# The order of two pairs of products, the merge of the branches and the sums of weights in a one-core attention and FFN block

## The chip, the core and the metric

The kernel runs on one core of a Trainium2 chip, in one launch. The metric is the device time of an execution in microseconds. Engines are named as the profile names them: PE (TensorE, matrix products), DVE (VectorE), ACT (ScalarE), POOL (GpSimd), and SP, whose queue here only issues DMA transfers. PEld is the loading of the stationary operand into PE.

## The reference

One layer of a streaming encoder: 512 tokens, 1024 channels, everything in float32. Two attention branches work on the same normalized input, are merged by sigmoid gates, and a gated feed-forward part with a short convolution follows.

```python
h = rmsnorm(x, norm_mix_g)
gq, gk, gv, gr, glr, fq, fk, fv, ff, g_gla, g_fox = jnp.split(h @ w_in, IN_OFFSETS, axis=-1)

log_a = log_sigmoid(glr @ gla_alpha_w2 + gla_alpha_b) / 16
o_gla = gla_chunked(gq * 64 ** -0.5, gk, gv, log_a)            # 4 heads, chunks of 64
o_gla = rmsnorm(o_gla, gla_out_norm_g) * silu(gr)

fqh, fkh = rmsnorm(fq, fox_q_norm_g), rmsnorm(fk, fox_k_norm_g)   # 8 heads of 64
o_fox = fox_attention(fqh, fkh, fv, log_sigmoid(ff + fox_forget_b))

y = sigmoid(g_gla + gate_b[0]) * (o_gla @ w_gla_branch) \
    + sigmoid(g_fox + gate_b[1]) * (o_fox @ w_fox_branch)
x = x + y @ w_out

a, val = jnp.split(rmsnorm(x, norm_ffn_g) @ w_up, 2, axis=-1)
x = x + (gelu(causal_dwconv(a, conv_w, conv_b)) * val) @ w_down
return rmsnorm(x, norm_final_g)
```

GLA is the gated linear attention (names with `g`), FoX the forgetting attention (names with `f`); `gr` is the output gate of GLA and is called `gz` in the kernel.

## The kernel before

**Exact products.** Every float32 product is made of three matmuls on a type of lower precision (`mm3`, lines 331 to 335): an operand is split into a rounded part and a remainder, and high by high, high by low and low by high are added in PSUM. Weights come from memory in pieces of 128x1024 float32, 512 KB each. Each piece is split when its turn is near (`split_next`): ACT makes `wh`, a cast of the loaded `raw` (line 298), and DVE makes `wl`, the difference of the two (line 299). Three pieces are held split at a time (`NW`). All pieces stand in one fixed list, `recipes`; a piece's number there is its time in the program.

**Fewer products.** Most large products are done by the 7 products of Strassen's method, numbered 1 to 7, over a 2x2 blocking. For this, some weights have to be added to one another. Such sums are not made by an engine: an accumulating DMA on POOL's queue adds a second matrix into the buffer (lines 306 and 310, through `dma_behind`). `dma_behind` first issues on POOL a tiny copy, `tick`, of one column of the split weights that have to be done before (line 314), and then the DMA (line 316).

**Loading.** SP issues the plain loads in the order of the list, each as soon as its buffer is free. `behind(n, "load" | "sum" | "add", ...)` ties transfers to the split of piece n. The weights of the down projection are also summed, in four arrays in memory, `wsum[0]` to `wsum[3]`: 24 copies on SP's queue (`COPY_AT`: at which piece each is issued) and 24 additions on POOL's (`ADD_AT`, `LATE_ADDS`).

**The work around the change.** In order of time:
1. The GLA inputs and four early tiles of the merge gates (`gate_tile(put_early(i))`), which are multiplied by `rb`, the factor of the first norm, and written to memory in `early` (line 692).
2. `pair_stage` (line 743), first for FoX keys and values (`kf`, `vf`), then for FoX queries and the output gate (`qf`, `gz`). One run of it computes a pair of products that share their input by Strassen's products in the order `PAIR`, 14 pieces of 12 matmuls (128x512) twice over. Product 5 comes first, its weights being a sum of two loads, then 1, 3, 6, 2, 7, 4. `pair_done` evicts: `left` is normalized per head (`qk_norm`, from `kssq` or `qssq`), `right` is scaled, and `final` is called for each of its four tiles; in the second run that is `silu` (line 870), a sigmoid on ACT, a product with it on POOL (line 873) and one into `ons`, the normalized GLA output, on DVE (line 874).
3. `fill()` lets the second run come to its end; then `transpose_heads` (line 876) transposes `ons` in two halves on PE.
4. FoX attention, with the remaining tiles of the gates put between its parts. `RUNS` tells for each key block how many steps of gate work go ahead of which part.
5. The merge (lines 1160 to 1193): for each of 8 tiles c, the two branch products are made, multiplied by the sigmoids of the gates `zg[c]` and `zf[c]`, added on POOL, and split into the operands of the output product (`halve`). The four early tiles come back from memory as `zd`.
6. The output product, whose product 5 reads a sum in the buffer `zr` (`OSUM` gives the tiles at which its load and its sum are issued), then the feed-forward part, and at its end a reload `xo<-x2d` of the residual on POOL's queue, tied by `dma_behind(last_lo, x2t, x2d)` to the split of the last large product.

The instructions are put on each engine in an order that a scheduler finds from the program; each engine then runs its own list in that order.

Of the kernel before, what the change touches and what calls it, by code (L numbers as in the profile page):

```python
# [86 lines left out]
def hybrid_kernel(ctx: ExitStack, tc, xT, xt, wp, wu, wd, wf, wn, pp, aw2, fing, out):  # L87
# [136 lines left out]
    for r in range(2):  # L224
        behind(KD + 1, "load", at_kv[5, r])
        behind(KD + 3 + r, "sum", at_kv[5, r], at_kv[1, r])
        behind(at_kv[7, r], "load", at_qr[5, r])
        behind(at_kv[2, 1] + r, "sum", at_qr[5, r], at_qr[1, r])
# [464 lines left out]
    def put_early(i):  # L693
        def put(ps):
            z = gpool.tile([P, T], F32, tag="sq", name="early", bufs=2)
            nc.vector.tensor_mul(out=z, in0=ps, in1=rb)
# [47 lines left out]
    def pair_stage(ssq, left, right, final=lambda tt: None):  # L744
        banks = {}
        for p, r in PAIR:
# [3 lines left out]
            for t2 in range(2):  # L750
                if r == 0 and new:
# [11 lines left out]
                if r == 1:  # L763
                    pair_done(p, t2, ps, ssq, left, right, final)
# [1069 lines left out]
```

## Time and profile before

| | |
|---|---|
| time, median of 3 runs | 721.43 us (719.76 to 723.34) |
| profiled execution: time / span | 720.45 / 718.7 us |
| mean granted clock of TensorE | 0.991 |
| busy: PE, DVE, ACT, POOL | 686.5, 553.7, 442.2, 153.5 us |
| idle of PE | 718.7 - 686.5 = 32.2 us |
| moved by DMA | 149.05 MB, 207 GB/s on average |

The span is the time from the first to the last instruction of the profiled execution. PE is busy nearly throughout, so the places of interest are the gaps in its work. In the timeline a row has start and duration, engine, line, operation, output and inputs with their shapes, and in brackets the idle time of the engine just before it and who ended it. The line of a weight split is always 298 or 299, so what it belongs to follows from the time and the buffer.

### The profile page before, as it was taken

How to read it: one execution, taken by the hardware profiler on the slowest of the kernel's cores; microseconds unless marked ns; L12 is line 12 of the kernel's file. 1: busy time of each engine (PE TensorE's matmuls, PEld its weight loads, DVE VectorE, ACT ScalarE, POOL GpSimd, SP SyncE). 2: the span in 40 equal slices, each digit the busy share in tenths (PEclk: the TensorE clock that was granted, in tenths of full speed). 3: DMA queues.
4: the chain of work that ended last, by engine and by line, in shares of the span. 5: the costliest groups of instructions: out<-in, count | busy, mean ns of one | idle time of the engine just before them, and what ended most of it. 6: DMA issues, size and time to landing. Idle time of an engine off the chain costs nothing.

```text
span 718.7 us, 10670 instructions
## 1 busy us (share of the span) xinstructions
PE 686.5 (96%) x3851; PEld 583.1 (81%) x3851; DVE 553.7 (77%) x876; ACT 442.2 (62%) x712; POOL 153.5 (21%) x206
## 2 busy tenths in 40 slices
PE   9999999897899999998899999999999999799996
PEld 6788888685678877876788999999999998588885
DVE  6776858679567776558769999888989879667884
ACT  8487374556767877624575766665665567355663
POOL 1134111104232211433100122111121204400112
PEclk9999999999999999999999999999999999899999
DMA  8789959875767767687895689999999988986543
GB/s 316 267 219 314 306 113 246 175 196 136 202 182 188 197 151 184 171 231 190 216 285 142 135 205 208 234 223 217 202 206 206 215 186 233 305 251 201 176 148 117
DMA packets 48633, 149.05 MB, mean 207 GB/s; under 512 B 5668, under 2 KB 9660, under 8 KB 48452
## 3 DMA queue, kind: packets, MB, share of 16 engines
q1 hardware_dynamic: 32452, 95.61, 38.9%
q0 software_dynamic: 12960, 47.72, 37.3%
q10 hardware_dynamic: 3168, 5.05, 2.0%
q8 instruction: 30, 0.49, 0.3%
q14 instruction: 23, 0.19, 0.1%
HBM read 143.09 MB, written 28.33 MB: 239 GB/s over the span
## 4 chain that ended last, share of the span: by engine, by line
PE 68%; DVE 10%; DMA 9%; ACT 8%; issue 3%; POOL 2%; DVEq 0%; ACTq 0%; POOLq 0%
PE ps_mm L334 12%; PE ps_mm L333 12%; PE ps_mm L335 12%; PE ps_wide L1476 8%; PE ps_wide L1478 4%; PE ps_wide L333 4%; PE ps_wide L335 4%; PE ps_wide L334 4%; DMA zr<-in_wp_dram 4%; DVE wl L299 4%; ACT wh L298 2%; DMA early<-early 2%; DMA rawp<-in_wp_dram 1%; ACT pr L1016 1%; DMA xo<-x2d 1%
## 5 line engine op out<-in xcount | busy, mean ns | idle before, releaser
L298 ACT CAST wh<-rawx 128x1024 fp32r<-128x1024 f32 x75 | 76.0, 1013 | 60.9 <-PE ps_mm L334 32.3
L333 PE MATMUL ps_mm<-xw,wh 128*128 128x256 f32 (+1 forms) x296 | 101.0, 341 | 0.1
L334 PE MATMUL ps_mm<-xw,wh 128*128 128x256 f32 (+1 forms) x296 | 99.2, 335 | 0.0
L335 PE MATMUL ps_mm<-xw,wl 128*128 128x256 f32 (+1 forms) x296 | 99.1, 335 | 0.0
L299 DVE TENSOR_TENSOR wl<-rawx,wh 128x1024 fp32r<-128x1024 f32 x75 | 88.2, 1177 | 12.9 <-ACT wh L298 12.9
L299 DVE TENSOR_TENSOR wl<-raw,wh 128x1024 fp32r<-128x1024 f32 x58 | 71.4, 1233 | 11.6 <-ACT wh L298 10.6
L298 ACT CAST wh<-raw 128x1024 fp32r<-128x1024 f32 x58 | 60.8, 1049 | 25.2 <-PE ps_mm L335 9.6
L333 PEld LDWEIGHTS ps_mm<-xw,wh 128*128 128x128 f32 x296 | 56.7, 192 | 7.4 <-issue 1.4
L335 PEld LDWEIGHTS ps_mm<-xw,wl 128*128 128x128 f32 x296 | 56.7, 191 | 5.6
L334 PEld LDWEIGHTS ps_mm<-xw,wh 128*128 128x128 f32 x296 | 56.7, 192 | 5.1 <-DVE xw L1265 0.2
L299 DVE TENSOR_TENSOR wl<-rawz,wh 128x1024 fp32r<-128x1024 f32 x31 | 38.1, 1233 | 16.1 <-ACT wh L298 16.0
L306 POOL DMA_DIRECT2D rawx<-in_wu_dram x30 | 26.0, 867 | 111.6 <-DVE wl L299 76.8
L1476 PE MATMUL ps_wide<-xo,wh 128*128 128x512 f32 x192 | 48.1, 392 | 0.0
L334 PE MATMUL ps_mm<-wl,xw 128*128 128x512 f32 x88 | 35.8, 407 | 6.8 <-DVE wl L299 6.8
L333 PE MATMUL ps_mm<-xc,wh 128*128 128x256 f32 (+1 forms) x128 | 42.0, 328 | 0.0
L334 PE MATMUL ps_mm<-xc,wh 128*128 128x256 f32 (+1 forms) x128 | 41.5, 324 | 0.0
L335 PE MATMUL ps_mm<-xc,wl 128*128 128x256 f32 (+1 forms) x128 | 41.4, 324 | 0.0
L314 POOL COPY tick<-wl 128x1 f32<-128x1 f32 x38 | 19.8, 520 | 100.4 <-DVE wl L299 98.0
L298 ACT CAST wh<-rawz 128x1024 fp32r<-128x1024 f32 x31 | 32.3, 1046 | 12.6 <-PE ps_mm L335 6.5
L1476 PEld LDWEIGHTS ps_wide<-xo,wh 128*128 128x128 f32 x192 | 34.5, 189 | 6.2
L335 PE MATMUL ps_mm<-wh,xw 128*128 128x512 f32 x88 | 35.3, 401 | 0.0
L333 PE MATMUL ps_mm<-wh,xw 128*128 128x512 f32 x88 | 35.1, 400 | 0.0
(500 smaller groups left out, 1871.2 us busy)
## 6 DMA issues: line engine op xcount, KB each, us to landing
rawx<-in_wu_dram POOLq DMA_DIRECT2D x40, 512.0 KB, 7.2
rawz<-in_wp_dram SPq DMA_DIRECT2D x30, 512.0 KB, 6.3
raw<-in_wp_dram SPq DMA_DIRECT2D x20, 512.0 KB, 4.7
wsum<-in_wd_dram SPq DMA_DIRECT2D x20, 512.0 KB, 9.2
rawx<-in_wu_dram SPq DMA_DIRECT2D x20, 512.0 KB, 4.7
raw<-in_wu_dram SPq DMA_DIRECT2D x20, 512.0 KB, 5.0
rawx<-wsum SPq DMA_DIRECT2D x12, 512.0 KB, 4.5
wsum<-in_wd_dram POOLq DMA_DIRECT2D x10, 512.0 KB, 8.7
```

The costliest lines, as they stand in the source:

```text
L298: nc.scalar.copy(out=hi[:, :m], in_=raw[:, :m])
L299: last_split[:] = [nc.vector.tensor_sub(out=lo[:, :m], in0=raw[:, :m], in1=hi[:, :m].bitcast(F32))]
L306: nc.gpsimd.dma_start(raw, recipes[i][0], accum_op=ALU.add)
L314: now = nc.gpsimd.tensor_copy(out=tick, in_=lo[:, 0:1].bitcast(F32))
L333: mm(ps, lhsT=ah, rhs=bh, start=start, stop=False, **k)
L334: mm(ps, lhsT=ah, rhs=bl, start=False, stop=False, **k)
L335: mm(ps, lhsT=al, rhs=bh, start=False, stop=stop, **k)
L1016: nc.scalar.activation(out=p, in_=p, func=AF.Exp, scale=-1.0, bias=nm, accum_out=rs)
L1476: mm(ps[:, i], lhsT=wh[:, c], rhs=both[p][:, k], start=first and k == 0, stop=False, skip_group_check=True)
L1478: mm(ps[:, i, 0], lhsT=wl[:, c], rhs=both[p][:, k, 0], start=False, stop=k == KH - 1, skip_group_check=True,)
```

## The change

The change is in which pair comes first, in when things are merged and summed, and in the engine of one eviction. No product is added or left out.

1. **Pairs.** FoX queries and output gate come first, keys and values second. The second run has the order `PAIR2`: product 1 ahead of product 5. The PSUM banks of the first two sets are taken at the start of a run.
2. **Heads.** `silu` runs in the first of the two runs. The transposes of `ons` are put into the second run, the first half after 2 of its steps and the other after 6 more (`HEADS_AT`).
3. **Early gates.** `put_early` copies with ACT; the product with `rb` is made on DVE when a tile comes back, at the start of the merge.
4. **RUNS.** In two entries one step of gate work moves from ahead of a part to behind it.
5. **Sums of the down weights.** The last 6 copies are issued at pieces 20 to 22 (before: 44 to 54). The last 6 additions, which were issued at the last pieces of the program, go to pieces 56 to 63; the 18 others are spread over 44 to 55.
6. **Merge.** The sum and the splits of tile c-1 are issued behind the products of tile c. The loads and sums of `zr` move from tiles 4, 5, 6, 7 to 5, 6, 6, 7.

```diff
-    (7, "t2", 3, "v0", 3, "t3"),
+    (6, "t2", 4, "v0", 3, "t3"),
...
-    (7, "t8", 3, "v2", 3, "t9"),
+    (6, "t8", 4, "v2", 3, "t9"),
...
+HEADS_AT = (2, 6)
...
-COPY_AT = [8 + i * 2 // 3 for i in range(18)] + [44 + 2 * i for i in range(6)]
-ADD_AT = [44 + i for i in range(12)] + [56 + i * 3 // 2 for i in range(6)]
-LATE_ADDS = 6
+COPY_AT = [8 + i * 2 // 3 for i in range(18)] + [20 + i // 2 for i in range(6)]
+ADD_AT = [44 + i * 2 // 3 for i in range(18)] + [56 + i * 3 // 2 for i in range(6)]
...
-OSUM = (4, 5)
+OSUM = (5, 6)
 PAIR = ((5, 0), (5, 1), (1, 0), (1, 1), (3, 0), (3, 1), (6, 0), (6, 1), (2, 0), (7, 0), (7, 1), (2, 1), (4, 0), (4, 1))
+PAIR2 = PAIR[2:4] + PAIR[:2] + PAIR[4:]
...
-    at_kv = pair_recipes(16, 12, ("rawz", "rawp", "raw"))
-    at_qr = pair_recipes(20, 8, ("rawz", "raw", "rawp"))
+    at_qr = pair_recipes(20, 8, ("rawz", "rawp", "raw"), PAIR)
+    at_kv = pair_recipes(16, 12, ("rawz", "raw", "rawp"), PAIR2)
...
-        behind(at_branch[OSUM[0] + 2 * r], "load", at_out[5, r])
-        behind(at_branch[OSUM[1] + 2 * r], "sum", at_out[5, r], at_out[1, r])
+        behind(at_branch[OSUM[0] + r], "load", at_out[5, r])
+        behind(at_branch[OSUM[1] + r], "sum", at_out[5, r], at_out[1, r])
...
-    parts_at([at_last[1 + i] for i in range(LATE_ADDS)], adds_at, ((3, wsum[1]),))
...
-            nc.vector.tensor_mul(out=z, in0=ps, in1=rb)
+            nc.scalar.copy(out=z, in_=ps)
...
-        banks = {}
-        for p, r in PAIR:
+        banks = {name: [pmm() for _ in range(2)] for name in "zx"}
+        for p, r in pair:
...
-    work += [gate_tile(put_early(i)) for i in range(NEARLY)] + [pair_stage(kssq, kf, vf)]
+    work += [gate_tile(put_early(i)) for i in range(NEARLY)] + [
+        pair_stage(PAIR, qssq, qf, lambda: late["gz"], silu)
+    ]
...
-    work += [pair_stage(qssq, qf, gz, silu)]
+    fill(18)
+    work += [pair_stage(PAIR2, kssq, kf, lambda: vf)]
+    for u in range(2):
+        fill(HEADS_AT[u])
+        transpose_heads(u)
     fill()
-    for u in range(2):
-        transpose_heads(u)
...
         nc.sync.dma_start(zg[i], early[:, i])
+        nc.vector.tensor_mul(out=zg[i], in0=zg[i], in1=rb)
...
+        if c > 0:
+            merge(c - 1)
         if c in HELD:
             held.append(piece())
+    merge(KD - 1)
```

Three places show what the scheduler made of it. The first is PE around the end of the second run of `pair_stage`. Of the kernel before, the rows show the last gate matmuls ahead of the attention, with the second half of the transposes of `ons` (the first half stands 17 matmuls ahead, right behind the run's last matmul):

```order
L334 MATMUL ps_mm<-xw,wh 128x512
L882 MATMUL ps_ax<-ident,ons 128x128 x8
L335 MATMUL ps_mm<-xw,wl 128x512
L333 MATMUL ps_mm<-xc_110,wh 128x512
L334 MATMUL ps_mm<-xc_110,wh 128x512
L335 MATMUL ps_mm<-xc_110,wl 128x512
L333 MATMUL ps_mm<-xc_111,wh 128x512
L334 MATMUL ps_mm<-xc_111,wh 128x512
L335 MATMUL ps_mm<-xc_111,wl 128x512
L967 MATMUL ps_lg<-ident,kf 128x128 x4
L977 MATMUL ps_lg<-ident,qf 128x128 x4
L1004 MATMUL ps_lg<-kh,qh 128x128 x2
```

Of the change, the same place (the transposes of `kf` and `qf` now have 12 gate matmuls on either side):

```order
L333 MATMUL ps_mm<-xw,wh 128x512
L334 MATMUL ps_mm<-xw,wl 128x512
L972 MATMUL ps_lg<-ident,kf 128x128 x4
L982 MATMUL ps_lg<-ident,qf 128x128 x4
L332 MATMUL ps_mm<-xw,wh 128x512
L333 MATMUL ps_mm<-xw,wh 128x512
```

And of the change, the second half of the transposes of `ons` inside the second run (the matmuls around it are those of `pair_stage`):

```order
L332 MATMUL ps_mm<-wh,htz 128x512
L333 MATMUL ps_mm<-wl,htz 128x512
L334 MATMUL ps_mm<-wh,lmz 128x512
L885 MATMUL ps_ax<-ident,ons 128x128 x8
L332 MATMUL ps_mm<-wh,hqg 128x512
L333 MATMUL ps_mm<-wl,hqg 128x512
```

The transposes have left the place ahead of the attention.

The second place is DVE at the start of the merge; `ogl` are the remainders of the transposed GLA output, which PE's first products of the merge read. Before:

```order
L1159 TENSOR_TENSOR held<-ogr_115,ogh_2922 128x512
L1159 TENSOR_TENSOR ogl_2946<-ogr_116,ogh_2923 128x512
L955 TENSOR_TENSOR zg_1702<-ps_mm,rb 128x512
L1159 TENSOR_TENSOR ogl_2949<-ogr_117,ogh_2924 128x512
L299 TENSOR_TENSOR wl<-raw,wh 128x1024
L1159 TENSOR_TENSOR ogl_2952<-ogr_118,ogh_2925 128x512
```

In the change:

```order
L1165 TENSOR_TENSOR held<-ogr_115,ogh_2934 128x512
L1165 TENSOR_TENSOR ogl_2962<-ogr_116,ogh_2935 128x512
L960 TENSOR_TENSOR zg_1709<-ps_mm,rb 128x512
L1165 TENSOR_TENSOR ogl_2965<-ogr_117,ogh_2936 128x512
L1159 TENSOR_TENSOR zd<-zd,rb 128x512
L1165 TENSOR_TENSOR ogl_2968<-ogr_118,ogh_2937 128x512
L1159 TENSOR_TENSOR zd<-zd,rb 128x512 x3
L298 TENSOR_TENSOR wl<-raw,wh 128x1024
L1200 TENSOR_TENSOR zd<-ps_mm,zd 128x512
```

Four products of `zd` with `rb` have come in, the first of them ahead of the last `ogl`; the split `wl` has gone behind them.

The third place is the end of POOL's list: what follows the last accumulating DMA into the up weights (`wsum3` is the last array of sums, `wl_6004` in the list before and `wl_6020` in the changed one the split that `last_lo` names). Before:

```order
L306 DMA rawx_5546<-in_wu_dram 128x1024
L314 COPY tick_90<-wl_5984 128x1
L316 DMA wsum3_72<-wsum1_70 128x1024
L314 COPY tick_90<-wl_6044 128x1
L316 DMA wsum3_72<-wsum1_70 128x1024
L314 COPY tick_90<-wl_6064 128x1
L316 DMA wsum3_72<-wsum1_70 128x1024
L314 COPY tick_90<-wl_6004 128x1
L316 DMA xo2_6100<-x2d_2918 128x4096
L314 COPY tick_90<-wl_6004 128x1
L316 DMA xo2_6100<-in_fing_dram 128x1024
L314 COPY tick_90<-wl_6106 128x1
```

In the change:

```order
L305 DMA rawx_5564<-in_wu_dram 128x1024
L313 COPY tick_90<-wl_6020 128x1
L315 DMA xo2_6112<-x2d_2930 128x4096
L313 COPY tick_90<-wl_6020 128x1
L315 DMA xo2_6112<-in_fing_dram 128x1024
```

The additions into `wsum3` have left this place, and the reload of the residual follows the up weights directly.

More of the change, by code (lines that the diff above doesn't have):

```diff
@@ L224, in hybrid_kernel @@
     for r in range(2):
[L225 to L228, printed above, removed]
+        behind(KD + 1, "load", at_qr[5, r])
+        behind(KD + 3 + r, "sum", at_qr[5, r], at_qr[1, r])
+        behind(at_qr[7, r], "load", at_kv[5, r])
+        behind(at_qr[2, 1] + r, "sum", at_kv[5, r], at_kv[1, r])
         for at in (at_kv, at_qr):
@@ L742, in pair_operand, with pair_stage @@
         return xh[j * K2 + k][:, t], xl[j * K2 + k][:, t]
-    def pair_stage(ssq, left, right, final=lambda tt: None):
-        banks = {}
-        for p, r in PAIR:
+    def pair_stage(pair, ssq, left, right, final=lambda tt: None):
+        banks = {name: [pmm() for _ in range(2)] for name in "zx"}
+        for p, r in pair:
             name = {5: "z", 3: "z", 1: "x", 2: "x", 6: "y", 7: "y", 4: "y"}[p]
@@ L750, in pair_stage @@
             for t2 in range(2):
-                if r == 0 and new:
+                if r == 0 and p == 6:
                     banks.setdefault(name, []).append(pmm())
@@ L763, in pair_stage @@
                 if r == 1:
[L764 removed]
+                    pair_done(p, t2, ps, ssq, left, right(), final)
                 yield
@@ L795, in pair_done, with silu @@
             final(2 + t2)
+    def silu(tt):
+        gz, ons = late["gz"], late["ons"]
+        sg = gpool.tile([P, 512], F32, tag="sq", name="sg", bufs=2)
+        nc.scalar.activation(out=sg, in_=gz[:, tt], func=AF.Sigmoid)
+        nc.gpsimd.tensor_mul(out=sg, in0=gz[:, tt], in1=sg)
+        nc.vector.tensor_mul(out=ons[:, tt], in0=ons[:, tt], in1=sg)
     for qb in range(NT):
@@ L868, in hybrid_kernel @@
             pair_split((3, 6, 7)[tt], last_dve, ("qg", "kg", "fgs")[tt], ("e2", None, None)[tt])
-    def silu(tt):
-        sg = gpool.tile([P, 512], F32, tag="sq", name="sg", bufs=2)
-        nc.scalar.activation(out=sg, in_=gz[:, tt], func=AF.Sigmoid)
-        nc.gpsimd.tensor_mul(out=sg, in0=gz[:, tt], in1=sg)
-        nc.vector.tensor_mul(out=ons[:, tt], in0=ons[:, tt], in1=sg)
     def transpose_heads(u):
@@ L904, in hybrid_kernel @@
                 )
+    late["gz"] = gpool.tile([P, NT, 512], F32, tag="vg", name="gz")
     for u in range(2):
@@ L924, in hybrid_kernel @@
     rsqrt_mean(rg, gssq.rearrange("p u a b c -> p (u a b c)"), 16, 1.0 / GDV, gpool, "rg")
-    ons = gpool.tile([P, NT, 512], F32, tag="prev", name="ons")
+    ons = late["ons"] = gpool.tile([P, NT, 512], F32, tag="prev", name="ons")
     for u in range(2):
@@ L1160, in hybrid_kernel, with merge @@
     held = []
-    for c in range(KD):
-        w = piece()
-        pg = pmm()
-        feature_tile(pg, w, ogh, ogl, nk=GH)
-        pf = pmm()
-        feature_tile(pf, w, oth, otl, w0=GH, nk=GH)
+    def merge(c):
         z = zf[c]
-        sigmoid(zg[c], zg[c], bias=col(C_GB + c))
-        last_sigmoid = sigmoid(z, z, bias=col(C_GB + KD + c))
-        nc.vector.tensor_mul(out=zg[c], in0=pg, in1=zg[c])
-        nc.vector.tensor_mul(out=z, in0=pf, in1=z)
         if c < KD // 2:
@@ L1191, in hybrid_kernel @@
             halve(o24, k, z)
+    for c in range(KD):
+        w = piece()
+        pg = pmm()
+        feature_tile(pg, w, ogh, ogl, nk=GH)
+        pf = pmm()
+        feature_tile(pf, w, oth, otl, w0=GH, nk=GH)
+        z = zf[c]
+        sigmoid(zg[c], zg[c], bias=col(C_GB + c))
+        last_sigmoid = sigmoid(z, z, bias=col(C_GB + KD + c))
+        nc.vector.tensor_mul(out=zg[c], in0=pg, in1=zg[c])
+        nc.vector.tensor_mul(out=z, in0=pf, in1=z)
+        if c > 0:
+            merge(c - 1)
         if c in HELD:
             held.append(piece())
+    merge(KD - 1)
     x2 = [[opool.tile([P, T], F32, tag="ot", name="x2t", bufs=2 * GH) for _ in range(2)] for _ in range(NT)]
```

6 lines of the change are left out of this document (3 added, 3 removed).

## The prediction

> **What bounds the kernel now.** I read the first part of the page, then the list of who waited for whom on TensorE, then the timelines of the engines around each wait.
>
> ```profile
> PE 686.5 (96%) x3851; PEld 583.1 (81%) x3851; DVE 553.7 (77%) x876; ACT 442.2 (62%) x712; POOL 153.5 (21%) x206
> PE ps_mm L334 <- DVE wl L299: 8.4, 5, 3.7
> PE ps_ax L882 <- DVE ons L874: 5.3, 2, 3.3
> PE ps_mm L333 <- DVE zg L1170: 2.1, 2, 1.3
> PE ps_lg L1063 <- DVE pl L1045: 1.8, 2, 0.9
> ```
>
> TensorE is busy 686.5 of 718.7 us, so everything that can be won without taking matmuls away lies in 718.7 - 686.5 = 32.2 us of idle time, and in the stretches where its clock is low. The change keeps the number of large matmuls. The question is therefore which of the waits above it ends, and which new ones it makes. The four rows (us in total, times, longest) hold 17.6 of the 32.2 us. They belong to five places, taken in order of time below, with rows of the timeline: start and duration in us, the instruction, and in brackets the idle time before it and what ended it. All sums are made against the profiled execution, 720.45 us with a span of 718.7; that execution is 1 us below the median of the runs shown (721.43), inside their spread.
>
> **1. The early gates, 60 to 90 us.** Four evictions of early gate tiles move from VectorE, as products with `rb`, to ScalarE, as copies.
>
> ```profile
> 84.66 0.69 DVE L696 TENSOR_TENSOR early<-ps_mm,rb 128x512 f32<-128x512 f32 x1 [0.71 <-DMA early<-early]
> 87.15 0.68 PE L900 MATMUL ps_ax<-vg,sc 128*128 128x128 f32 x4 [0.95 <-DVE prev L863]
> ```
>
> The last of them holds VectorE for 0.71 + 0.69 us, ahead of the chain of `prev`, for which TensorE waits 0.95 us. Taken off that queue, 1.4 us are freed and the 0.95 us should go: **-0.9** (0 to -0.95). ScalarE pays four copies of 0.67 us (the 2.67 for four of that size in section 4); it is busy 62% of the span and nothing of TensorE waits for it here.
>
> **2. From the first half of the pair work to the second.** Before, the second stage starts with product 5, whose weights are the sum of two loads.
>
> ```profile
> 126.96 0.50 PE L334 MATMUL ps_mm<-wl,htz 128*128 128x512 f32 x1 [0.81 <-DVE wl L299]
> 130.78 0.50 PE L334 MATMUL ps_mm<-wl,htz 128*128 128x512 f32 x1 [0.80 <-DVE wl L299]
> 135.43 0.50 PE L334 MATMUL ps_mm<-wl,xw 128*128 128x512 f32 x1 [1.63 <-DVE wl L299]
> 128.36 1.06 ACT L298 CAST wh<-rawp 128x1024 fp32r<-128x1024 f32 x1 [2.77 <-DMA rawp<-in_wp_dram]
> ```
>
> Three waits, 3.24 us, and the ScalarE row shows why: the cast waited 2.77 us for the accumulating DMA into `rawp`. With `PAIR2` the stage starts with product 1, a plain load, and the two sums are wanted two pieces later. That is 24 matmuls, 5.0 us by the window of 605 to 610 below, against 2.77 of lateness, so the DMA is covered. But the split of the first piece now stands on VectorE behind the first product of `silu`, which waits for POOL. The nearest row is the 1.63 above, a split held up in VectorE's queue. I take one such wait a little shorter, 1.4, and one of 0.5 us in place of the three: **-1.3** (from -3.2 to +1.5, three waits of 1.6 each).
>
> **3. From the second half to the logits, 168 to 190 us.**
>
> ```profile
> 170.43 0.88 PE L882 MATMUL ps_ax<-ident,ons 128*128 128x128 f32 x6 [2.03 <-DVE ons L874]
> 178.48 1.17 PE L882 MATMUL ps_ax<-ident,ons 128*128 128x128 f32 x8 [3.27 <-DVE ons L874]
> 183.71 0.33 PE L1004 MATMUL ps_lg<-kh,qh 64*128 64x128 f32 x2 [1.56 <-ACT qh L979]
> 172.71 2.81 POOL L873 TENSOR_TENSOR sg<-gz,sg 128x512 f32<-128x512 f32 x2
> 172.33 3.23 DVE L376 TENSOR_TENSOR rq16w<-rq16w,rq16v 128x16 f32<-128x16 f32 x1
> 171.70 0.17 DVE L376 TENSOR_TENSOR rq16w<-rq16w,rq16v 128x16 f32<-128x16 f32 x1
> 166.12 0.67 DVE L670 TENSOR_REDUCE qssq<-fsq 128x8 f32<-128x512 f32 x1
> 163.80 2.40 DVE L680 TENSOR_TENSOR qf<-qf,rq 128x512 f32<-128x512 f32 x2
> 168.02 0.38 PE L882 MATMUL ps_ax<-ident,ons 128*128 128x128 f32 x2
> 176.44 1.29 DVE L680 TENSOR_TENSOR qf<-qf,rq 128x512 f32<-128x512 f32 x2
> 185.00:190.00 5.00, 4.85 (x24) 3.91 (x25) 2.74 (x16) 3.58 (x10) 0.20 (x1) 0.69 1.03 248
> ```
>
> At the end of stage 2 TensorE waits 2.03 + 3.27 us for `ons`, that is for sigmoid, POOL's product and VectorE's product of the last tiles, and then 1.56 us for `qh`, whose norm ran late in the same queues. VectorE's tiny step of 0.17 us took 3.23 at 172.33, beside POOL's two products (2.81). In the change these products belong to stage 1, and the transposes are taken in the middle of stage 2, after 2 and then 6 more steps, with 12 or more matmuls ahead of each, so `ons` is no longer waited for (some 2.5 us of cover per 12 matmuls). What stays is the norm of the keys. VectorE has two splits left ahead of it, ten steps of about 0.2 us and the products (1.29 for two). From the last sum of squares (done at 166.79, and 1.1 us sooner without POOL beside it, since the product at 163.80 took 2.40 where 1.29 is its time) that is 2.4 + 2.1 + 1.3 = 5.8 us: the norm is done at 171.5. Stage 2 ends at 168.02 and 12 gate matmuls cover 2.5, to 170.5. I take 1.0 us in place of 2.03 + 3.27 + 1.56 and the 0.7 of two short waits behind: **-6.5** (-4.5 to -7.5). The last row is of the view by windows (busy us of the five engines, then granted clock, DMA share, GB/s) and shows a granted 0.69 for the 5 us after these waits; (1 - 0.69) x 5 = 1.6 us. With nothing longer than 1 us ahead, that goes: **-1.6** (0 to -1.6).
>
> **4. The merge, 280 to 346 us.** Here the change adds a wait.
>
> ```profile
> 280.20 2.92 SPq L1153 DMA_DIRECT2D zd<-early  x4
> 287.66 2.67 ACT L1149 ACTIVATE zd<-zd,ppt 128x512 f32<-128x512 f32 x4 [3.15 <-DMA zd<-early]
> 285.26 0.68 DVE L1159 TENSOR_TENSOR ogl<-ogr,ogh 128x512 fp32r<-128x512 f32 x1
> 286.00 0.51 PE L334 MATMUL ps_mm<-ogl,wh 128*128 128x512 f32 x1 [0.52 <-DVE ogl L1159]
> 312.55 0.90 POOL L316 DMA_DIRECT2D zr<-in_wp_dram  x1 [6.76 <-DMA zr<-in_wp_dram]
> 317.73 0.47 PE L333 MATMUL ps_mm<-ogh,wh 128*128 128x512 f32 x1 [1.27 <-DVE zg L1170]
> ```
>
> The product with `rb` is now made when the early tiles come back, and the first of the four stands on VectorE ahead of the last `ogl`. The tiles land at about 287.6 (ScalarE's first row that was released by them). The product takes 0.69, `ogl` 0.68: TensorE, which needs `ogl` and stood from 285.48 (286.00 - 0.52), goes on at about 289.0. That is 3.5 us of idle in place of 0.52: **+3.0**. Would the clock fall too? After 3.27 and then 1.56 us of idle it fell to 0.69 (section 3), after 3.71 to 0.50 (section 5); after 2.03 alone no window fell. 3.5 lies between, so I count 2 us: **+2.0** (0 to 2.5). In the Trainium skill, "TensorE: Matmul & The Clock Gate", section "HAM oscillation — how this bites in real kernels", the rule is no idle gap of TensorE over some 3.4 us; by it this wait, worked out at 3.5, would cost the low clock, and by the page the sum keeps the 2 us. It speaks against this part of the change; the trace agrees as far as 3.71 did and 2.03 did not.
>
> In exchange, POOL stood 6.76 us behind the load of `zr`, with the sum of the fourth tile queued behind it; that made the 1.27, and 0.85, 0.22, 0.61 and 0.28 after it, 3.2 us in the same chain. The sums of the tiles now come ahead of that queue entry, and each merge has one more tile (5.4 us) to finish. I count **-4.5**: these 3.2 and some of the 1.7 us at the first product of the output weights. Bounds -1 and -5; the net of the merge is +0.5 (-2 to +4.5).
>
> **5. The tail, 594 to 635 us.** Six additions into the down weights leave POOL's queue here.
>
> ```profile
> 605.10 0.51 POOL L314 COPY tick<-wl 128x1 f32<-128x1 f32 x1 [2.47 <-DVE wl L299]
> 606.08 7.54 POOL L314 COPY tick<-wl 128x1 f32<-128x1 f32 x1
> 613.57 0.58 POOL L316 DMA_DIRECT2D xo<-x2d  x1
> 614.37 1.23 DVE L299 TENSOR_TENSOR wl<-raw,wh 128x1024 fp32r<-128x1024 f32 x1 [0.79 <-POOL tick L314]
> 615.67 1.23 DVE L299 TENSOR_TENSOR wl<-rawx,wh 128x1024 fp32r<-128x1024 f32 x1
> 622.39 1.29 DVE L1674 TENSOR_TENSOR xo<-xo,ps_wide 128x512 f32<-128x512 f32 x2 [5.49 <-DMA xo<-x2d]
> 615.65 0.50 PE L334 MATMUL ps_mm<-wl,xw 128*128 128x512 f32 x1 [1.49 <-DVE wl L299]
> 624.87 0.80 PE L334 MATMUL ps_mm<-wl,xw 128*128 128x512 f32 x1 [3.71 <-DVE wl L299]
> 605.00:610.00 5.00, 5.00 (x24) 4.14 (x23) 5.00 (x8) 2.67 (x6) 4.90 (x3) 1.00 1.02 243
> 625.00:630.00 5.00, 5.00 (x12) 3.95 (x13) 3.62 (x5) 0.46 (x1) 0.00 (x0) 0.50 1.06 246
> ```
>
> The reload `xo<-x2d` stands on POOL behind three of the additions. Its tick copy then took 7.54 us beside a VectorE that was busy for all of 605 to 610, the load went out at 613.57 and VectorE stood 5.49 us for it, with the next split behind: 3.71 us of TensorE, and 12 matmuls in the next 5 us where there are 24 at full clock, 2.5 us. Without the additions the same tick is due as soon as its split is done, some 7 us sooner. If it takes the 0.5 of the tick at 605.10, the load is issued by 602 and lands by 611 (8.7 us to landing, 622.39 - 613.57), ahead of 616.90, where VectorE wants it. The 0.79 at 614.37, a split behind that tick, goes as well. **-3.7 - 2.5 - 0.8 = -7.0** (0 to -7.0). The additions themselves run earlier, on other pieces of POOL's queue, at 0.5 us a tick.
>
> **6. What I count at nothing.** Two entries of `RUNS` move one step of filling from ahead of one run to behind the next: the same work stands ahead of what follows, and the 1.8 us of waits for `pl` hang on a chain of VectorE: 0 (-1.8, both gone, to +0.9, one more). Six copies into the down weights, 0.5 MB each, move to pieces 20 to 22.
>
> ```profile
> 95.00:100.00 5.00, 5.00 (x23) 4.13 (x22) 4.73 (x12) 3.69 (x5) 0.86 (x1) 1.00 0.17 16
> 105.00:110.00 5.00, 5.00 (x24) 4.14 (x23) 3.35 (x4) 2.24 (x3) 0.00 (x0) 1.00 1.06 198
> ```
>
> The DMA engines are 0.17 busy at 95 to 100 us, which is cover for half of the 3 MB (15 us at the 198 GB/s of the second row); from 105 on they are full. TensorE waits for no load there now. I take 0 (to +10).
>
> **Sum.** -0.9 - 1.3 - 6.5 - 1.6 + 0.5 - 7.0 = -16.8, so 720.45 - 16.8 = 703.7 us; I say 704.
>
> **The rivals.**
> - *The tick is starved all the same.* VectorE is as busy at 598 to 613 as before, and a tick took 7.54 us there; against it, the one at 605.10 took 0.51 in the same stretch. Then the load goes out near 613 again, the 7.0 us are lost, and the time is 711. The Trainium skill, "SBUF — State Buffer", section "SBUF: two separate sides", has VectorE and GpSimd share one pair of ports under an exclusive lock; by it a copy on POOL may wait for a run of VectorE's two-input operations, and the 7.54 us agree, while the 0.51 does not.
> - *The merge gives more back.* The wait for the early tiles falls on a later landing, TensorE's clock falls, and the loads of `zr`, of which there are now two in a chain, hold SP and the output pieces: the net is +4.5 in place of +0.5, so 708.
> - *The heads do not leave the path.* The transposes in stage 2 wait for `ons` as they did, with the same POOL products: half of the 8.1 us of section 3 stays, 708.
> - *Slower.* The six copies stand on SP ahead of the loads of the pair pieces. If these 3 MB, 15 us of full DMA, fall behind 105 us instead of the gap, the pieces' loads come late by up to 15 us, less the 3 to 5 us that they are ahead now: 10 us in stage 1, and again in stage 2, whose sums are accumulated on top of those buffers. Each such wait also costs the low clock, 2.5 us. 2 x 12.5 = 25 against 16.8: 728. It decides once pieces land over 9 us late; the 0.17 speaks against it.
>
> **How the numbers follow.** My case 0.68, at 704 with its bounds 697 to 708; starved tick 0.13, at 711; merge 0.07 and heads 0.05, at 708; slower 0.07, at 728 if it is full, near no change if half. The range of 697 to 714 takes in all but the last, with 3 us over the starved tick for copies that come a little late. A measurement of this kernel can tell about 0.5%, 3.6 us: faster by more than that 0.89, within it 0.05, slower 0.06.
>
> **What would show it.** Right: no wait for `ons` and clock 1.00 through the start of the logits; the `xo` load issued before 605 or so and no TensorE wait over 1 us after 610; one wait of 3 to 4 us for `ogl` at the merge's start, and no 6.76 on POOL ahead of the fourth tile. Wrong: a tick of several us on POOL near 600; splits in stages 1 and 2 that wait for DMA; a second wait in the merge as long as the first.

## The result, and the profile after

The changed kernel takes 711.3 us (median; 708.3 to 712.5) against 720.6 us before: a ratio of 0.9864, interval 0.9816 to 0.9912. That is 9.3 us faster, inside the range given, but little over half of the 16.8 us that were worked out. The profiled execution, at 712.52 us with a span of 710.8, is the slowest of the four; sums over stages and waits are made in its time below, and for every other run in that of its own profiled execution.

The first part of the page and the list of who waited for whom on TensorE (us in total, times, longest) now read:

```profile
PE 686.8 (97%) x3851; PEld 585.7 (82%) x3851; DVE 553.3 (78%) x876; ACT 444.6 (63%) x716; POOL 147.8 (21%) x206
PE ps_mm L333 <- DVE ogl L1165: 3.8, 2, 3.5
PE ps_mm L332 <- DVE zg L1200: 3.4, 1, 3.4
PE ps_lg L1068 <- DVE pl L1050: 2.5, 2, 1.6
PE ps_lg L1068 <- ACT ph L1049: 2.0, 1, 2.0
PE ps_mm L333 <- DVE wl L298: 2.0, 2, 1.3
```

The 5.3 us for `ons` and most of the 8.4 us for `wl` are gone. At the head of the list stand waits that the kernel before did not have or had at 0.5 to 1.3 us. TensorE's busy time is the same, but busy time counts matmuls at the low clock as well: three stretches now run at it (195 to 210, 280 to 290 and 325 to 340 us), where the kernel before has two (185 to 195 and 620 to 635). The rows of the timeline of TensorE that cut the run into four, for the kernel before:

```profile
281.42 0.51 PE L333 MATMUL ps_mm<-ogh,wh 128*128 128x512 f32 x1
345.92 0.51 PE L334 MATMUL ps_ax<-wl,oh 128*128 128x512 f32 x1 [0.76 <-DVE wl L299]
```

and for the changed one:

```profile
174.23 0.33 PE L1009 MATMUL ps_lg<-kh,qh 64*128 64x128 f32 x2
274.40 0.51 PE L332 MATMUL ps_mm<-ogh,wh 128*128 128x512 f32 x1
346.30 0.50 PE L333 MATMUL ps_ax<-wl,oh 128*128 128x512 f32 x1 [0.76 <-DVE wl L298]
```

The first logits stood at 183.71 before. So the spans of the four stages, and what the prediction had for each, are:

| stage | before | after | measured | predicted |
|---|---|---|---|---|
| to the first logits | 183.71 | 174.23 | -9.5 | -0.9 - 1.3 - 6.5 = -8.7 |
| attention, to the first product of the merge | 97.71 | 100.17 | +2.5 | -1.6 |
| merge, to the output product's second piece of a split | 64.50 | 71.90 | +7.4 | +0.5 |
| from there to the end | 372.78 | 364.50 | -8.3 | -7.0 |
| sum | 718.7 | 710.8 | -7.9 | -16.8 |

Two stages did what was expected, and 2.1 us more in all; the two others missed it by 11 us. The experiments below look for the cause of each.

### The profile page after: what moved, and what is told of

Same layout as the page of the kernel before. It is cut to its first block, busy times and chain, and to the rows that moved or that the text cites. A ratio compares the mean times of both kernels' runs of the same rounds, so it can differ in the third digit from the quotient of the medians.

```text
span 710.8 us, 10664 instructions
## 1 busy us (share of the span) xinstructions
PE 686.8 (97%) x3851; PEld 585.7 (82%) x3851; DVE 553.3 (78%) x876; ACT 444.6 (63%) x716; POOL 147.8 (21%) x206
## 4 chain that ended last, share of the span: by engine, by line
PE 74%; DMA 9%; DVE 8%; ACT 4%; issue 3%; POOL 2%; SPq 0%; ACTq 0%; POOLq 0%; DVEq 0%
PE ps_mm L332 14%; PE ps_mm L333 14%; PE ps_mm L334 13%; PE ps_wide L1489 8%; PE ps_wide L332 4%; PE ps_wide L333 4%; PE ps_wide L334 4%; PE ps_wide L1491 4%; DMA zr<-in_wp_dram 4%; DMA cb<-nct 4%; DVE wl L298 3%; PE ps_lg L1068 1%; ACT pr L1021 1%; ACT wh L297 1%; DMA zd<-early 1%
## 5 line engine op out<-in xcount | busy, mean ns | idle before, releaser
L313 POOL COPY tick<-wl 128x1 f32<-128x1 f32 x38 | 13.8, 362 | 114.7 <-DVE wl L298 113.5
L332 PE MATMUL ps_mm<-wh,xw 128*128 128x512 f32 x88 | 34.3, 390 | 0.0
L334 PE MATMUL ps_mm<-wh,xw 128*128 128x512 f32 x88 | 34.3, 389 | 0.0
```

The costliest lines, as they stand in the source:

```text
L313: now = nc.gpsimd.tensor_copy(out=tick, in_=lo[:, 0:1].bitcast(F32))
L332: mm(ps, lhsT=ah, rhs=bh, start=start, stop=False, **k)
L334: mm(ps, lhsT=al, rhs=bh, start=False, stop=stop, **k)
```

## The experiments

Each of the first four takes the changed kernel and edits one part of it.

**The product with `rb` behind the last `ogl`.**

```diff
     for i in range(NEARLY):
         zg[i] = bpool.tile([P, T], F32, tag="zd", name="zd", bufs=NEARLY)
         nc.sync.dma_start(zg[i], early[:, i])
-        nc.vector.tensor_mul(out=zg[i], in0=zg[i], in1=rb)
...
-        nc.vector.tensor_sub(out=ogl[h], in0=ogr[h], in1=ogh[h].bitcast(F32))
+        last_ogl = nc.vector.tensor_sub(out=ogl[h], in0=ogr[h], in1=ogh[h].bitcast(F32))
+    for i in range(NEARLY):
+        with tc.issue_after(last_ogl.ins):
+            nc.vector.tensor_mul(out=zg[i], in0=zg[i], in1=rb)
```

> The changed kernel (711.3 us) with one edit: the four products of the early tiles with rb are made behind the last ogl on VectorE, no longer ahead of it. Theory: the 3.47 us wait for ogl at the merge's start and the low clock behind it (0.58 and 0.73 in the two windows of 5 us) are the price of that one product's place; the wait falls to 0.5 us or so, the clock stays at 1.00, and the time falls by 3.0 + 2 to 3 = 5 to 6 us, to 705.5. Rival: the first sigmoid needs the same early tile, so the wait only moves to the first merge products; TensorE stands as long at the second or third tile and the time stays within 2 us of 711.3.

Measured: 703.7 us (ratio to before 0.9728, 0.9695 to 0.976), 7.6 us below the changed kernel. In the changed kernel the timelines of VectorE and TensorE and the view by windows (busy us of five engines, granted clock, DMA share, GB/s) show what the place costs:

```profile
280.33 0.69 DVE L1159 TENSOR_TENSOR zd<-zd,rb 128x512 f32<-128x512 f32 x1 [3.14 <-DMA zd<-early]
280.94 0.68 DVE L1165 TENSOR_TENSOR ogl<-ogr,ogh 128x512 fp32r<-128x512 f32 x1
281.68 0.80 PE L333 MATMUL ps_mm<-ogl,wh 128*128 128x512 f32 x1 [3.47 <-DVE ogl L1165]
280.00:285.00 5.00, 3.32 (x8) 2.65 (x9) 4.67 (x7) 3.94 (x7) 0.00 (x0) 0.58 0.27 105
285.00:290.00 5.00, 5.00 (x18) 3.99 (x17) 0.86 (x2) 1.55 (x2) 1.27 (x1) 0.73 0.31 107
```

VectorE stood 3.14 us for the early tile with `ogl` behind it, TensorE 3.47. With the edit:

```profile
280.28 0.50 PE L333 MATMUL ps_mm<-ogl,wh 128*128 128x512 f32 x1 [0.54 <-DVE ogl L1164]
280.00:285.00 5.00, 4.72 (x21) 3.88 (x22) 3.89 (x7) 3.73 (x7) 0.00 (x0) 1.00 0.74 281
```

The wait and the low clock are gone, and the wait does not turn up later: the products with `rb` had time behind `ogl`. The second wait of the merge (3.43 us for `zg`) went as well, which had not been expected from this edit; 0.59 us of it is left. So the 7.6 us are the price of both waits, not of the first alone.

**One load into `zr` instead of two.** Each of the two pieces that go into `zr` is loaded once by the look-ahead and once more by its own entry. (SP issues four loads into `zr` in the changed kernel; in the kernel before it issued three, at 300.97, 315.77 and 321.30 us.)

```diff
             if what == "load":
-                load_raw(i)
+                if i not in raws:
+                    load_raw(i)
```

> The changed kernel with one edit: a load that has been issued already is not issued again (two of the four loads into zr are left out; they bring in the same weights twice). Theory: POOL stands 6.30 and 8.57 us for the second load of each pair, and the sums of tiles 4 and 5 behind it; without them the sums are made in time, the 3.43 us wait for zg at 329.5 and the half clock behind it (0.50 in one window) go, and the time falls by 3.4 + 2.5 = 6 us, to 705.5. Rival: POOL stands for the first load as well, because SP issues it late; then one wait of 6 us stays on POOL and TensorE's wait falls by less than half, to 709 or so.

Measured: 705.5 us (0.9755, 0.9714 to 0.9797). SP's, POOL's and TensorE's timelines of the changed kernel:

```profile
297.87 12.97 SPq L268 DMA_DIRECT2D zr<-in_wp_dram  x2
314.35 0.90 POOL L315 DMA_DIRECT2D zr<-in_wp_dram  x1 [6.30 <-DMA zr<-in_wp_dram]
318.80 0.33 SPq L268 DMA_DIRECT2D zr<-in_wp_dram  x1
325.27 0.88 POOL L315 DMA_DIRECT2D zr<-in_wp_dram  x1 [8.57 <-DMA zr<-in_wp_dram]
325.88 1.56 POOL L1179 TENSOR_TENSOR zg<-zg,zg 128x512 f32<-128x512 f32 x1
329.47 0.80 PE L332 MATMUL ps_mm<-held,oh 128*128 128x512 f32 x1 [3.43 <-DVE zg L1200]
330.00:335.00 5.00, 5.00 (x13) 3.63 (x12) 3.39 (x6) 2.27 (x4) 2.85 (x2) 0.50 0.50 98
```

The last load into `zr` is issued at 318.80, and POOL stands for its landing until 325.27. The sum of tile 5 (the sixth; tiles count from 0) runs behind that, and VectorE and TensorE behind the sum. With the second loads left out, POOL's two entries read:

```profile
311.17 0.90 POOL L316 DMA_DIRECT2D zr<-in_wp_dram  x1 [2.63 <-DMA zr<-in_wp_dram]
313.81 0.88 POOL L316 DMA_DIRECT2D zr<-in_wp_dram  x1 [0.17 <-issue]
```

and TensorE has no wait for `zg` at all, though the first wait of the merge (3.70 us) is still there. So either edit ends the second wait. In the first experiment the same four loads still hold POOL for 3.12 and 6.38 us, and are over by 315.93. But the chain of loads and the first wait together are not the whole cause: the next two experiments keep both, and the second wait is shorter in them. How the first wait makes the chain longer was not tried apart.

**The additions at their old density.**

```diff
-ADD_AT = [44 + i * 2 // 3 for i in range(18)] + [56 + i * 3 // 2 for i in range(6)]
+ADD_AT = [44 + i for i in range(12)] + [56 + i * 3 // 2 for i in range(6)]
...
-    parts_at(ADD_AT, adds_at, ((0, b11), (2, b12), (1, wsum[0]), (3, wsum[1])))
+    parts_at(ADD_AT, adds_at, ((0, b11), (2, b12), (1, wsum[0])))
...
+    parts_at([at_step[4 + i, 1] for i in range(6)], adds_at, ((3, wsum[1]),))
```

> The changed kernel with the additions into the down weights at the density of before: 12 at pieces 44 to 55, 6 at 56 to 63, and the last 6 in the middle of the feed-forward part instead of near the end. Theory: the waits for ph and pl at 198.6 and 200.7 us (2.04 + 1.59) come from the loads of cb, 15.3 us to landing beside five additions; with fewer additions these loads land in 9 to 11 us, the waits fall to 1 us, the clock stays at 1.00 (now 0.50 for 5 us), and the time falls by 2.6 + 2.5 = 5 us, to 706. Rival: the loads of cb are late because they are issued late and wanted sooner, whatever runs beside them; the waits stay at 3 us or more and the time within 1.5 us of 711.3.

The last six, which have no place at the old density, go into the feed-forward part. Measured: 708.6 us (0.98, 0.9755 to 0.9844); its runs (705.1 to 711.4) overlap with those of the changed kernel (708.3 to 712.5), so what the edit does is read from the profile. In the changed kernel, POOL's and TensorE's timelines and one window in the attention read:

```profile
188.10 0.42 POOL L638 TENSOR_TENSOR cb<-cb,negm 128x128 f32<-128x128 f32 x1 [10.25 <-DMA cb<-nct]
193.75 1.41 POOL L638 TENSOR_TENSOR cb<-cb,negm 128x128 f32<-128x128 f32 x3 [1.30 <-DMA cb<-nct]
198.60 0.54 PE L1068 MATMUL ps_lg<-ph,v 128*128 128x512 f32 x1 [2.04 <-ACT ph L1049]
200.73 0.80 PE L1068 MATMUL ps_lg<-pl,v 128*128 128x512 f32 x1 [1.59 <-DVE pl L1050]
200.00:205.00 5.00, 4.27 (x15) 3.99 (x16) 2.29 (x5) 0.89 (x2) 1.36 (x3) 0.50 1.04 234
```

With the additions at the old density (four of them between 166 and 178 us, where the changed kernel has six):

```profile
188.47 1.98 POOL L640 TENSOR_TENSOR cb<-cb,negm 128x128 f32<-128x128 f32 x5 [0.41 <-DMA cb<-nct]
198.09 0.50 PE L1070 MATMUL ps_lg<-pl,v 128*128 128x512 f32 x1 [0.87 <-DVE pl L1052]
200.00:205.00 5.00, 5.00 (x34) 3.99 (x33) 4.68 (x8) 3.60 (x7) 1.81 (x5) 1.00 0.51 111
```

The last of the six sums of `cb` ends at 190.45 (188.47 + 1.98) in place of 195.16, the wait for `ph` is gone and `pl` is back at the 0.87 of before. The loads of `cb` of 192 and 128 KB that are issued from 177 us on take 10.4 us to landing, where they take 15.3 in the changed kernel and in the kernel before 8.3 and 8.6. For these waits the mechanism is the one expected. The time fell by 2.7 us and not by 5, and the edit did more than was expected of it, which the profiled execution (705.1, the fastest of the four) shows: the attention is 4.8 us shorter, the part from the output product on, in which six additions now stand, 2.0 us longer, and the merge 4.7 us shorter. There the first wait is still 3.17 us and POOL waits 4.52 and 7.15 us for the loads of `zr`, but the second wait has shrunk without a low clock:

```profile
PE ps_mm L334 <- DVE zg L1203: 1.6, 2, 1.0
330.00:335.00 5.00, 4.04 (x16) 2.49 (x15) 3.66 (x8) 3.01 (x6) 0.67 (x1) 1.00 1.00 306
```

Which of these gains the slower three executions lack is open.

**The old `RUNS`.**

```diff
-    (6, "t2", 4, "v0", 3, "t3"),
+    (7, "t2", 3, "v0", 3, "t3"),
...
-    (6, "t8", 4, "v2", 3, "t9"),
+    (7, "t8", 3, "v2", 3, "t9"),
```

> The changed kernel with the old RUNS: one step of gate work (three matmuls, 0.7 us) goes back in front of t2 and of t8. Theory: the total of work ahead of v0 and v2 is the same, and the waits for ph and pl hang on the loads of cb; the time is unchanged, 711.3 within 1 us. Rival: the move of RUNS is what brings TensorE to v0 too early; then the waits at 198.6 and 200.7 shrink by at least half and the clock stays up, 707.

Measured: 709.7 us (0.9808, 0.9772 to 0.9844), 1.6 us below the changed kernel and inside the spread of its runs. The waits for `ph` (1.9 us) and `pl` (2.8 in all) stay: `RUNS` is not what makes them. The first wait of the merge stays too (3.45 us), but the second is 1.93 and 0.99 us with the clock at 1.00, though POOL still waits 6.12 and 7.15 us for the loads of `zr`; the last landing holds POOL until 322.74 in place of 325.27. So a landing 2.5 us earlier went with a shorter wait in two parts and no low clock.

**All three edits together**, with the six additions in the feed-forward part.

> The changed kernel with the edits of e1, e2 and e3 together. Theory: three separate losses (the place of one product with rb; the density of the additions beside the loads of cb; the second load into zr). e1 measured 703.7, which also ended the second merge wait (0.6 us left), so e2 adds little to e1; e3's part is the waits at v0 (2.46 + 1.79 in e1's profile, against 0.9 at old density) and 5 us at a clock of 0.56: 3.3 + 2.5 us. The time is 703.7 - 5.5 = 698, TensorE's mean clock 0.995 or more. Rival: the places share one cause (an overlap of DMA traffic, or the clock), so the gains don't add up: 702 or more.

Measured: 697.5 us (0.9673, 0.9616 to 0.973), below both kernels. The time is the 698 that was expected. The three gains taken singly are 7.6 + 5.8 + 2.7 = 16.1 us, against 13.8 together, since each of the three edits ends or shortens the same second wait. No window of 5 us ahead of the end has a clock below 0.985.

The next three take the kernel before and add one part of the change, or the changed kernel and leave all but one.

**The tail alone**, in the kernel before:

```diff
-    parts_at([at_last[1 + i] for i in range(LATE_ADDS)], adds_at, ((3, wsum[1]),))
+    parts_at([at_step[4 + i, 1] for i in range(LATE_ADDS)], adds_at, ((3, wsum[1]),))
```

> The kernel before with one edit: the last 6 additions into the down weights are issued in the middle of the feed-forward part, no longer at its end. Theory: the 7.54 us tick ahead of the reload of the residual, 3.71 + 0.79 us of TensorE and 2.5 us of low clock hang on these additions alone; the ratio to before is (720.5 - 7.0) / 720.5 = 0.990, and the reload is issued by 605 us. Rival: VectorE's run of work starves the tick as it did, the reload goes out past 612 us, and the ratio is 0.998 or more.

Measured: 717.1 us (0.9939, 0.9904 to 0.9974), half of the 7 us. The reload was issued at 605.51 and both waits of the tail are gone, but new waits stand where the additions went: 0.72 and 0.47 us for splits at 521 and 533, 1.32 for `joint` at 540, 2.5 us in all.

**The pairs and heads alone** (parts 3 to 6 of the change undone).

```diff
-            nc.scalar.copy(out=z, in_=ps)
+            nc.vector.tensor_mul(out=z, in0=ps, in1=rb)
...
-OSUM = (5, 6)
+OSUM = (4, 5)
...
-        if c > 0:
-            merge(c - 1)
...
-    merge(KD - 1)
...
+    parts_at([at_last[1 + i] for i in range(LATE_ADDS)], adds_at, ((3, wsum[1]),))
```

> The changed kernel with parts 3 to 6 of the change undone: only the order of the pairs and the place of the heads differ from before. Theory: the three waits between the pairs shrink from 3.24 to 2.0 us, the waits ahead of the logits from 7.5 to 0.3 us, and the low clock behind them goes (1.6 us): 10 us in all, less what the loads of cb cost because the attention starts sooner (0 to 3 us at the old density of the additions); a ratio of 0.986 to 0.990. Rival: the whole gain of this part is given back in the attention, which has its own pace from the loads of cb on; a ratio of 0.995 or more.

Measured: 710.1 us (0.9861, 0.9796 to 0.9926): by itself this part is worth as much as the whole change. The waits between the pairs are 1.35 and 0.63, none over 0.45 us stands between them and the logits, and the attention waits 0.91 + 0.98 us at `v0` against 2.04 + 1.59 with the denser additions. With the early products still on VectorE, its profile shows a wait of 4.24 us for `prev` at 90.55. The profiled execution, at 714.77, is the slowest of the four; the others took 709.8 to 710.4, so that wait need not be in them.

**The later merge alone**, in the kernel before.

```diff
-OSUM = (4, 5)
+OSUM = (5, 6)
...
+        if c > 0:
+            merge(c - 1)
...
+    merge(KD - 1)
```

> The kernel before with part 6 of the change alone: the merge of a tile one tile later, loads and sums of zr at tiles 5, 6, 6, 7. Theory: without the product with rb in front of ogl, this removes the 1.27 + 0.85 + 0.22 us at the merge and some of the waits at the first output products, 2 to 3 us, a ratio of 0.996 or so. Rival: the second load of zr that this part adds holds POOL for 6 to 8 us even so, a wait for zg of 2 us or more takes the place of the 1.27, and the ratio is 1.000 or above.

Measured: 720.35 us, ratio 1.0001 (0.9964 to 1.0037), the rival's figure. POOL stands 3.95 and 6.66 us for the loads of `zr`, and TensorE waits 1.06, 0.98 and 0.59 us for `zg` in place of 1.27, 0.85 and 0.22: no single wait of 2 us, as the rival had it, but no less in all.

The last four look for the best place for the additions. All have the edits of the first two experiments and the old density elsewhere.

**Beside the output product.**

```diff
-    parts_at([at_step[4 + i, 1] for i in range(6)], adds_at, ((3, wsum[1]),))
+    parts_at([66 + 2 * i for i in range(6)], adds_at, ((3, wsum[1]),))
```

> e5 (697.5 us) with the last 6 additions at pieces 66, 68 to 76, beside the output product, in place of the feed-forward part. Theory: e5 still paid 2 to 3 us for additions in the feed-forward part (waits of 0.77, 0.55 and 0.76 for splits between 514 and 546 us); beside the output product they lie in cover, the stretch from the first output product's second matmul to the end falls from 367.8 to 364.5 or 365 us, and the time is 694.5. Rival: the additions now hold the sums of zr and rawz on POOL, and the output product waits for them: 697.5 or more.

Measured: 701.6 us (0.9729, 0.9671 to 0.9786). The rival's time held, and its wait. Nothing waits for the sums of the down weights, but ScalarE's cast of a `rawz` piece waited 5.14 us for its DMA, VectorE's sums into `x2t` behind it, and TensorE for those:

```profile
348.27 1.04 ACT L299 CAST wh<-rawz 128x1024 fp32r<-128x1024 f32 x1 [5.14 <-DMA rawz<-in_wp_dram]
351.37 0.77 PE L335 MATMUL ps_mm<-wh,oh 128*128 128x512 f32 x1 [5.09 <-DVE x2t L1239]
```

The additions did not hold that DMA back on POOL: the two accumulating loads into `rawz` are issued at 332.71 and 334.73, against 332.78 and 334.50 in the last experiment below, which has no additions here. But they take 11.3 us to landing (median of the two), against 6.5 there.

**In the same kernel, the first twelve earlier**, in the second run of the pairs.

```diff
-ADD_AT = [44 + i for i in range(12)] + [56 + i * 3 // 2 for i in range(6)]
+ADD_AT = [33 + i for i in range(12)] + [56 + i * 3 // 2 for i in range(6)]
```

> e9 with the first 12 additions at pieces 33 to 44, in the second run of the pairs, so that none runs beside the loads of cb. Theory, if the attention waits for loads of cb because of the additions: the waits of 1.1 us for pl at 198 and 243 us go or shrink to 0.9 as in the kernel before, nothing is lost in the pairs, whose DMA share is about 0.8: 694 or so. Rival: the accumulating loads of the pairs (8 us to landing) and their ticks stand behind the additions, splits come late, and the second run of the pairs waits 2 us or more: 697 or more.

Measured: 712.0 us (0.9884, 0.9816 to 0.9952), worse by 10 us. ScalarE's cast waited 8.30 us for an accumulating load of the pairs, and TensorE for the cast:

```profile
169.32 1.04 ACT L299 CAST wh<-rawp 128x1024 fp32r<-128x1024 f32 x1 [8.30 <-DMA rawp<-in_wp_dram]
170.41 0.55 PE L335 MATMUL ps_mm<-wh,xc 128*128 128x512 f32 x1 [4.22 <-ACT wh L299]
```

The two accumulating loads are issued at 143.82 and 145.63 us, against 143.49 and 145.06 in the run before, but take 19.8 us to landing (median of the two) against 5.9. The 0.88 us for `pl` at the two places of the attention stayed as they were, though the loads of `cb` of 192 and 128 KB ahead of the first place now land in 5.5 us; so the wait there, at least, does not come from late loads of `cb`.

**The six where the kernel before had them.**

```diff
-    parts_at([66 + 2 * i for i in range(6)], adds_at, ((3, wsum[1]),))
+    parts_at([at_last[1 + i] for i in range(6)], adds_at, ((3, wsum[1]),))
```

> e9 with the last 6 additions put back where the kernel before had them, at the last pieces, 3 of them ahead of the reload of the residual. Theory: the tail of before comes back whole: a tick of 7.5 us, the reload near the end of VectorE's run of work, a wait of 3.7 us and the low clock: 7 us over e9. Rival (what e6 measured): the tail is worth 3.5 us only, and the change's gain there came from somewhere else.

Measured: 702.3 us (0.9736, 0.9688 to 0.9784). The tail of before is back, with the same tick:

```profile
589.34 7.55 POOL L316 COPY tick<-wl 128x1 f32<-128x1 f32 x1
596.83 0.58 POOL L318 DMA_DIRECT2D xo<-x2d  x1
598.91 0.50 PE L336 MATMUL ps_mm<-wl,xw 128*128 128x512 f32 x1 [2.23 <-DVE wl L300]
608.22 0.50 PE L336 MATMUL ps_mm<-wl,xw 128*128 128x512 f32 x1 [2.20 <-DVE wl L300]
```

That it is no slower than the run with the six beside the output product (701.6), which has none of these waits, is the 5.09 us that one had instead; the two cannot be set against each other for the tail's price.

**And three pieces later**, so that all six stand behind the reload.

```diff
-    parts_at([at_last[1 + i] for i in range(6)], adds_at, ((3, wsum[1]),))
+    parts_at([at_last[4 + i] for i in range(6)], adds_at, ((3, wsum[1]),))
```

> e11 with one shift: the last 6 additions three pieces later, so that all stand behind the reload of the residual on POOL's queue; as many additions in the tail, none ahead of the reload. Theory: what the tail of before pays for is only the place of the reload's tick behind three additions, which puts it beside VectorE's run of work; the reload goes out near 590 us, the waits of 2.23 and 2.20 us and the low clock go, and the time is 702.3 - 6 = 696, below the 697.5 of e5. Rival: it is the traffic of the additions beside the reload, or beside the last splits, that makes TensorE wait; then waits of 4 us or more stay near 600 and the time is 700 or more.

Measured: 695.35 us (0.961, 0.957 to 0.965), the fastest of all, 16 us below the changed kernel and 27.7 below the kernel before beside it (723.0). The same six additions in the same tail, but the reload ahead of them:

```profile
582.42 0.78 POOL L316 COPY tick<-wl 128x1 f32<-128x1 f32 x1 [10.14 <-DVE wl L300]
583.14 0.56 POOL L318 DMA_DIRECT2D xo<-x2d  x1
```

The tick takes 0.78 us in place of 7.55 and TensorE's longest wait from there on is 0.43. One addition's tick now takes 4.33 us in its turn, and nobody waits for it. Nor did the additions slow the reload: it took 8.7 us to landing in the kernel before and 8.8 in the run above, with three additions issued right behind it, and 10.2 in the changed kernel, with none. So the tail paid for the reload's place in POOL's queue, not for the traffic of the additions. The price is 702.3 - 695.4 = 6.9 us by the medians; it is 9 by the ratios, and 370.33 - 365.53 = 4.8 from the output product on in the two profiled executions.

## Why the prediction was right or wrong

The direction and the range held; the size did not, by 9 us of span. That the 711 measured is also the figure of the starved tick is chance: the tick was not starved, and what cost the 9 us lies in the attention and the merge. The range took it in with 2.7 us to spare. Of the signs of being wrong that were named, one came: a second wait in the merge as long as the first (3.43 and 3.47 us). Step by step:

- **Early gates, -0.9.** Right. No wait for `prev` is left; ScalarE now stands 2.39 us for the buffer of the early tiles, and TensorE does not wait for it. The pairs alone, with the products left on VectorE, had 4.24 us of wait there in one execution, so beside the new order of the pairs this part may be worth more; it was not tried apart.
- **Between the pairs, -1.3.** Right in kind and size: two waits of 1.35 and 0.66 us against 1.4 and 0.5.

```profile
126.39 0.50 PE L333 MATMUL ps_mm<-wl,xw 128*128 128x512 f32 x1 [1.35 <-DVE wl L298]
170.80 0.33 PE L972 MATMUL ps_lg<-ident,kf 128*128 128x128 f32 x1 [0.28 <-DVE kf L679]
```

- **To the logits, -6.5.** Right, a little small: 0.28 us of wait for the norm of the keys where 1.0 was taken. The low clock at 185 us went too (-1.6). The pairs alone then measured a ratio of 0.9861, some 10 us, where the sum has -1.3 - 6.5 - 1.6 = -9.4 for them.
- **"The additions themselves run earlier, on other pieces of POOL's queue, at 0.5 us a tick."** This step failed. A tick was the wrong price: an addition moves 0.5 MB beside the loads of `cb`, and the denser ones made these loads late (15.3 us to landing against 10.4). In the changed kernel that is 2.04 + 1.59 us in place of 0.89 and 5 us at half the clock, (2.04 + 1.59 - 0.89) + 2.5 = 5.2 us, somewhat more than the 4.1 by which this stage missed its -1.6. The old density removed it.
- **The merge, "I count -4.5".** The wait for `ogl` came as worked out, 3.47 us against 3.5, and the low clock behind it cost more than the 2.0 counted: 8 matmuls in 3.32 us and then 18 in 5 where 24 in 5 us is full clock, some 2.9 us. The credit was taken back. The small waits did shrink (1.27, 0.85, 0.22, 0.61, 0.28, 0.90 and 0.76 became 0.28, 0.28, 0.42 and 0.76, that is 4.9 to 1.7 us), but one of 3.43 us came in their place. It was thought that sums "now come ahead of that queue entry"; the fourth does, but each entry now had a second load to wait for, and the sums from the sixth tile on stand behind the later entry as the fourth did before. The rival "the merge gives more back" had this mechanism and put +4.5 on it; +7.4 was measured, since the clock fell behind the wait of 3.43 us as well. Without the product with `rb` ahead of `ogl`, or without the second loads, the wait is gone; but it is also down to 0.99 + 0.60 and 1.93 + 0.99 us in two runs that keep both, so its full length took a late landing besides.
- **The tail, -7.0.** Right: TensorE has no wait over 1 us there, and the tick of the reload takes 0.78 us. The stage fell by 8.3; 0.7 of the 1.3 more is TensorE's wait of 1.49 us at 615.65, of which 0.8 was counted.

```profile
599.34 0.78 POOL L313 COPY tick<-wl 128x1 f32<-128x1 f32 x1 [10.14 <-DVE wl L298]
600.06 0.56 POOL L315 DMA_DIRECT2D xo<-x2d  x1
610.00:615.00 5.00, 5.00 (x24) 4.14 (x23) 5.00 (x8) 3.82 (x6) 0.00 (x0) 1.00 0.93 322
```

VectorE is busy for the whole of 595 to 620 us, and the rival of a starved tick expected 7 us there. The tick ran beside it in 0.78 us; why others took 7.54 and 4.33 beside the same kind of work was not found.
- **Copies at nothing.** No load of the pairs is waited for in the two runs of the pairs, by ScalarE's casts or by TensorE, so the rival of a slower kernel found no ground. They were not moved alone.
- **`RUNS` at nothing.** Undone, the median is 1.6 us lower with the times of the executions overlapping: not told from nothing.

## What to carry to other kernels

An accumulating DMA that is moved is not priced by its issue. Loads beside it landed later: 19.8 us after their issue in place of 5.9, 11.3 in place of 6.5, 15.3 in place of 10.4. (The first two go through POOL's queue like the additions, and whether the shared queue or the bytes delayed them was not told apart; the third, of `cb`, are on SP's queue.) And what stands on POOL behind an addition's tick has to wait. With the same six additions the kernel took 695.4, 697.5, 701.6 or 702.3 us by where they stood, and the best of the four places was behind the one transfer that the end waits for. Where an operation is moved onto a queue and waits there for a DMA, what matters is what stands behind it: one product of 0.7 us ahead of another that TensorE needed cost 7.6 us here, a later wait that it lengthened included, and nothing behind it. And a piece that is loaded twice can lie unseen until a neighbour moves, as the third load into `zr` of the kernel before did; a count of loads against pieces would have shown it.

## What had not been expected of the hardware

TensorE's low clock came after shorter waits than it had been counted for. After the same wait of 2.0 us for `ons`, the kernel before ran on at 1.00 and the one with the later merge alone at 0.67, in the same window of the two runs:

```profile
170.00:175.00 5.00, 4.57 (x23) 3.73 (x23) 4.86 (x8) 3.02 (x6) 4.26 (x6) 1.00 0.81 248
170.00:175.00 5.00, 5.00 (x19) 4.11 (x18) 4.79 (x8) 2.66 (x6) 3.93 (x5) 0.67 0.97 268
```

In the run that puts the six additions where the kernel before had them, a wait of 2.23 us at 598.91 was followed by a window at 0.70, and one of 2.20 at 608.22 by none below 1.00. Waits of 3.17, 3.43, 3.47, 4.22, 4.24 and 5.09 us were each followed by a window below 0.75. But the 3.27 of the kernel before was so only once 1.56 had come on top, and after the 3.25 in the same place of the run with the tail alone the windows stood at 0.87 and 0.79 until 0.83 and 0.92 us more had come. By the Trainium skill, "TensorE: Matmul & The Clock Gate", section "What's actually happening", the clock is set by activity in a window of about 3.4 us that runs freely, so when it falls depends on where a wait lies in it; that fits the two rows, while an idle gap of 2.0 us shows that one need not fill a whole window. A wait of 2 us is therefore worth 2 to 4 us here (an estimate: 2.0 + (1 - 0.67) x 5 = 3.7), and which, the profile of one execution does not tell beforehand.
